# Operand splits queued behind weight splits, the first up weights staged earlier, the norm's factor and the conv rows computed later

## The chip, the cores and the metric

One Trainium2 chip, one core of it. The metric is device microseconds of one execution of the whole program. Engines are called as the profile calls them: PE (matmul), DVE, ACT, POOL and SP, which here issues most loads and stores.

## What is computed

One decoder layer on 512 prompt rows and 32 sample rows (544 columns). After retention, attention and the output projection, which the change leaves alone but for the tail of the projection, comes the feed-forward part:

```python
hp = hp + mixer_output(ro, rg, so, ret_gn_w[l], w_o[l], hp.dtype)
...
hn = rmsnorm(h, ffn_norm_w)
up = jnp.einsum('btd,df->btf', hn, w_up)              # 2048 -> 2 * 5632
g, u = jnp.split(up, 2, axis=-1)
gp = jnp.concatenate([conv_buf.astype(g.dtype), g], axis=1)
gc = conv_b + sum(gp[:, j:j + T] * conv_w[j] for j in range(CONV_W))
y = jnp.einsum('btf,fd->btd', jax.nn.silu(gc) * u, w_down)   # 5632 -> 2048
return y, gp[:, -(CONV_W - 1):]                        # the last two rows: "conv rows"
```

`rmsnorm` multiplies by the weight and by a factor per row, rsqrt(mean of squares + eps); the kernel applies the factor after the up product.

## The kernel before

**Precision.** All large products are made of two-part numbers: `hi` is a rounded copy that ACT makes (`act.copy`, L150), `lo = src - hi` comes from DVE (L151). Both parts of both sides are split; a product is hi·lo + lo·hi + hi·hi, three matmuls for each k of 128 rows. `split` does the two instructions.

**Units.** The up and down projections run in units (`unit`, L1112). A unit multiplies a 2x2 block matrix of weights by a 2x2 block of operands with seven products instead of eight. In the order of the program they are b11, t1, t2, b21, t3, b22, t4. For each, the weights (a raw block, or a sum of raw blocks that DVE makes at L1132, L1135, L1142, L1146) are split into one of three `uhi`/`ulo` buffers, in turn, and then multiplied (`product`, L1092) by the split operand of the same name in `xop`. A product takes 24 matmuls with 8 k's and 21 with 7. The results leave PSUM through ACT copies (`tu`, `p5`, `us`) and DVE adds. Work of the neighbouring unit (`todo`) is put between the products: `run(1)` after b11, `run(6)` after t2, `run(2)` after b21, `run(3)` after b22.

**The stages.** The output projection's second half (L1025 to L1042) ends at its sixteenth pass, i = 15; each pass loads weights into `raw` (three buffers, as `whi` and `wlo` have, in the pool `wp`), splits them, multiplies, adds the residue (`x1`), scales, stores `x1`, makes the operands of the up units (`build_x`) and sums the squares in `ssq`. After it four wide splits make the operands of b21 and t4 from `C` (L1043 to L1045). The pools `tb1` (`t1k`, two `x1`, `sq2`) and `wp` are closed and `ua` lies where they were; `ub` lies where `C` was. Pools lay their buffers out in the order of first use: in `ua` `us`, `g`, `tu` come first (8.8 KB of a partition), then three `uraw` of 4 KB; `tb1` is 7.6 KB and `wp` lies above it. A buffer waits only for the old buffers that it overlaps. `rstd_ffn` computes the norm's factor: two matmuls with `onesD` over `ssq`, then Ln, Exp and five DVE instructions. It is in the first unit's `run(2)`.

44 up units follow (`up_pair`), each with its conv, gate and, every second one, `blocks`, which stores the down operands in DRAM (`hx_keep`). Then the down units: three chunks of 8, 7 and 7 k's, eight units each. At the last unit ahead of a chunk, after each product, `fill` loads the operand of that name for the next chunk into the `lo` buffer (POOL's queue, L1224) and splits it there in two steps of up to four k's. `conv_rows` transposes the conv rows on PE in the first chunk's units 1 to 5.

**Order.** The kernel is written in Tile: a scheduler orders each engine's instructions ahead of time by priority and by when it expects them ready. On the chip each engine runs its list strictly in that order. The order in the trace can so differ from the order in the source.

I name the four places where a stage ends: T1 (output projection to up), B2 (up to the first down chunk), B3 and B4 (to the second and third chunk). A name with a prime (b11', t1') is a product of the first unit behind such a place.

Of the kernel before, what the change touches and what calls it, by code (L numbers as in the profile page):

```python
# [106 lines left out]
def trunk_kernel(  # L107
# [39 lines left out]
        return wp.tile([128, 8, 128], F32, name="raw", tag="raw")  # L147

    def split(hi, lo, src, eng=dve):
        act.copy(out=hi, in_=src)  # L150
        eng.tensor_tensor(out=lo, in0=src, in1=hi.bitcast(F32), op=sub)  # L151

    def stage_half(load, q, eng=dve):
        raw = wraw()
# [871 lines left out]
    for i in range(KT):  # L1026
        m = i // 2 + 8 * (i % 2)
        acc = half_project(m, 1, A_hi[:, 0:8], A_lo[:, 0:8])
        x1 = tb1.tile([128, 2, HC], F32, name="x1", tag="x1", bufs=2)
        dve.tensor_tensor(out=x1, in0=acc, in1=C[:, m], op=add)  # L1030
        act.activation(out=C[:, m], in_=x1, func=AF.Copy, scale=ffnw[:, m:m + 1])
        sth(out=x1_keep[m], in_=x1)
        if i % 2 == 0:
            split_x("b11", m, C[:, m, 0])
        else:
            build_x(i // 2)
        if i == 0:
            act.activation(out=ssq, in_=x1, func=AF.Square)
        else:
            sq = tb1.tile([128, 2, HC], F32, name="sq2", tag="sq2", bufs=1)  # L1040
            act.activation(out=sq, in_=x1, func=AF.Square)
            pool.tensor_tensor(out=ssq, in0=ssq, in1=sq, op=add)  # L1042
    for u in range(2):  # L1043
        for k in range(0, 8, 4):
            split(A_hi[:, k:k + 4, u], A_lo[:, k:k + 4, u], C[:, k + 8:k + 12, u])  # L1045
    tst.close()
    wst.close()
    ost.close()


    ust, ust2, upst = ExitStack(), ExitStack(), ExitStack()
    ps = upst.enter_context(tc.tile_pool(name="ps3", bufs=2, space=PSUM, reuse_waits="tile"))
    ua = ust.enter_context(tc.tile_pool(name="ua", bufs=1, reuse_waits="tile"))
    cst.close()
    ub = ust2.enter_context(tc.tile_pool(name="ub", bufs=1, side="right", reuse_waits="tile"))

    def ring(name, shape, dtype, n_a, n_b):
        turn_ = [0]

        def take():  # L1060
            i = turn_[0] % (n_a + n_b)
            turn_[0] += 1
            p, n = (ua, n_a) if i < n_a else (ub, n_b)
            return p.tile(shape, dtype, name=name, tag=name, bufs=n)
        return take

# [5 lines left out]
    new_cv = ring("cv", [128, 562], F32, 0, 1)  # L1072
    new_tu = ring("tu", [128, 2, HC], F32, 1, 1)
    new_us = ring("us", [128, 2, 2, HC], F32, 1, 0)
    new_p5 = ring("p5", [128, HC], F32, 0, 1)
    new_tt = ring("tt", [128, 3, HC], F32, 0, 1)

    def rstd_ffn():
        vb, tb = new_g()[:, 0:544].rearrange("p (u c) -> p u c", u=2), new_cv()[:, 0:544].rearrange("p (u c) -> p u c", u=2)
        for u in range(2):  # L1080
            pm = small2(ps)
            pe.matmul(pm[:, :HC], lhsT=onesD, rhs=ssq[:, u, :], start=True, stop=True)
# [6 lines left out]
    def b44(a):  # L1089
        return a.rearrange("p u (b t) -> p u b t", t=4)  # L1090

    def product(bank, w, x, first, last, parts=None):  # L1092
        n = w.shape[1]
        hi, lo = new_hi()[:, :n], new_lo()[:, :n]
        split(hi, lo, w)
        xh, xl = xop[x]
        for ks in parts or (range(n),):
            for k in ks:
                pe.matmul(bank, lhsT=hi[:, k], rhs=xl[:, k], start=(first and k == 0), stop=False, skip_group_check=True)  # L1099
                pe.matmul(bank, lhsT=lo[:, k], rhs=xh[:, k], start=False, stop=False, skip_group_check=True)  # L1100
# [3 lines left out]
    def unit(load, us, todo, joined, sign=1.0, behind={}, parts=None):  # L1104


        def run(when):
            for part in todo.get(when, ()):
                part()

        def prod(*a):
            product(*a, parts=parts)  # L1112
# [5 lines left out]
        tu, p5 = new_tu(), new_p5()  # L1118

        def out(dst, src):  # L1120
            if sign == 1.0:
                act.copy(out=dst, in_=src)  # L1122
            else:
                act.activation(out=dst, in_=src, func=AF.Copy, scale=sign)  # L1124

        a11, a21, a22 = load(0, 0), load(1, 0), load(1, 1)
        prod(bx, a11, "b11", True, False)
        act.copy(out=tu[:, 0], in_=bx)
        run(1)
        n = a11.shape[1]  # L1130
# [12 lines left out]
        prod(bx, a21, "t3", False, False)  # L1143
        out(us[1], bx)
# [8 lines left out]
    ups = {}  # L1153

    def load_up(f):
        def load(i, q):
            raw = new_raw()
# [2 lines left out]
        return load  # L1160

    def up_pair(f, todo, behind={}):
        if f % 2 == 0:
            ups["us"] = new_us()
        us2 = ups["us"]
        us = us2[:, f % 2]
        g = new_g()

        def joined(zy, tu):
            pool.memset(g[:, 0:2], 0.0)  # L1170
            pool.tensor_copy(out=g[:, 514:562].rearrange("p (b x) -> p b x", x=6)[:, :, 0:2],
                             in_=stT[:, :, f].rearrange("p (b r) -> p b r", r=2))
# [4 lines left out]
            dve.tensor_tensor(out=gs, in0=gs, in1=b44(rstd_bc[:, :, 256:272]), op=mult)  # L1177

        def conv():
            pool.tensor_copy(out=co[:, 0:2, f], in_=g[:, 512:514])  # L1180
            pool.tensor_copy(out=co[:, 2:18, f].rearrange("p (b r) -> p b r", r=2), in_=g[:, 514:562].rearrange("p (b x) -> p b x", x=6)[:, :, 4:6])
            cv = ups["cv"] = new_cv()
# [5 lines left out]

        def gated():
            cv = ups["cv"]  # L1190
            dve.tensor_tensor(out=us, in0=us, in1=rstd_bc, op=mult)  # L1191
            dve.scalar_tensor_tensor(out=us[:, :, 0:256], in0=us[:, :, 0:256], scalar=-1.0, in1=halves_of(cv[:, 0:512]), op0=mult, op1=mult)
            uss = b44(us[:, :, 256:272])
# [2 lines left out]
        def blocks():  # L1196

            j = f // 2
            tt = new_tt()
            for op, src in ((0, us2[:, 0, 0]), (5, us2[:, 1, 1]), (3, us2[:, 1, 0])):  # L1200
                sth(out=hx_keep[op][:, j], in_=src)
# [6 lines left out]
            sth(out=hx_keep[6][:, j], in_=tt[:, 1])  # L1208
            sth(out=hx_keep[1][:, j], in_=tt[:, 2])

        unit(load_up(f), (us[:, 0], us[:, 1]), todo, joined, behind=behind, parts=None if f else (range(7), range(7, 8)))
        return {1: [conv], 6: [gated], 2: [blocks] if f % 2 else []}


# [2 lines left out]
    chunks = ((0, 8), (8, 7), (15, 7))  # L1217

    def fill(c, name):
        def go():  # L1220
            j0, n = chunks[c]
            hi, lo = xop[name]
            raw = lo.bitcast(F32)
            sth(out=raw[:, :n], in_=hx_keep[order7.index(name)][:, j0:j0 + n])  # L1224
            for h in range(0, n, 4):
                p = slice(h, min(h + 4, n))
                if name == "t2":
# [4 lines left out]
        return go  # L1232

    def fills(c):
        return {name: fill(c, name) for name in order7} if c < len(chunks) else {}

    def emit_y(m, y):
        yp = new_g()[:, 0:512].rearrange("p (c d) -> p c d", c=4)
# [12 lines left out]
    def down_pair(c, mp, todo):  # L1251
# [24 lines left out]
        unit(load, (y[:, 1, 0], y[:, 1, 1]), todo, joined, sign=-1.0, behind=fills(c + 1) if mp == 7 else {})  # L1276
        return {6: [finish_y if last else keep_y]}

    todo = {2: [rstd_ffn]}
    for f in range(FT):  # L1280
        todo = up_pair(f, todo, behind=fills(0) if f == FT - 1 else {})

    def conv_rows(q):
        def go():
            n = min(4, 18 - 4 * q)
            cob = new_g()[:FT, 0:512].rearrange("p (i c) -> p i c", c=128)
            pt = small2(ps)
            for i in range(n):
                pe.transpose(out=pt[:FT, 128 * i:128 * i + 128], in_=co[:, 4 * q + i, :], identity=ident)
# [49 lines left out]
```

## Time and profile before

| | us |
|---|---|
| median of 3 runs | 2242.22 (2238.29 to 2245.8) |
| profiled execution, its own time | 2239.99 |
| its span, first to last instruction | 2238.2 |
| PE busy | 2176.6 (97%) |
| DVE busy | 1630.1 (73%) |
| ACT busy | 1010.7 (45%) |
| POOL busy | 291.9 (13%) |
| mean granted TensorE clock | 0.986 of full speed |

The page cuts the span into 40 slices of 56 us. PE's busy digit is 9 in nearly all, DVE's is 8 through the up stage; the granted clock is 8 or 9 tenths in the first slices, in those around 760, 1710, 1910 and 2050 us, and at the end. Matmuls are pipelined and a busy PE isn't a PE at its peak, so the count of matmuls in a stretch says more than the busy time. DMA moves 128 GB/s in the mean; the highest slice, the first, has 289 GB/s, and a store of `x1` (272 KB) takes 2.4 us from issue to landing. Durations of single instructions include a tenth of a microsecond in which the next one already runs.

### The profile page before, as it was taken

Reading aid. Unit: us, or ns where it says so; the run is one execution under the profiler, and the core shown is the slowest. Engines: PE = TensorE matmul, PEld = TensorE weight load, DVE = VectorE, ACT = ScalarE, POOL = GpSimd, SP = SyncE. Lnnn points to the kernel's source line nnn. Section 1 sums busy time; section 2 is a strip of 40 time slices with the busy share of each in tenths; the row PEclk is TensorE's granted clock in tenths of the full one; section 3 lists DMA queues with packets and bytes.
Section 4 is the critical chain, followed back from the end, with each engine's and each line's share of the span. In section 5 each row is a group of like instructions: output and inputs, shape, how many; then the busy total and the mean of one; then the engine's idle time right before and its main releaser. Section 6 shows DMA issues by size and latency. Waiting matters only on the chain.

```text
span 2238.2 us, 42004 instructions
## 1 busy us (share of the span) xinstructions
PE 2176.6 (97%) x17159; PEld 2139.1 (96%) x17159; DVE 1630.1 (73%) x2457; ACT 1010.7 (45%) x1612; POOL 291.9 (13%) x463
## 2 busy tenths in 40 slices
PE   7999999999999799999999999999998999898998
PEld 7999999999999799999999999999998999898998
DVE  5555557875437778888888888888888767767775
ACT  5122235566215544444444444444445445445444
POOL 1000000000003212122122122122122101001000
PEclk8999999999999899999999999999998999999999
DMA  9333343324644343343443443434436656557553
GB/s 289 100 97 94 87 88 77 82 67 120 130 115 136 112 124 114 113 145 107 121 137 113 124 125 116 133 114 126 124 116 224 149 128 194 139 131 221 140 150 98
DMA packets 452656, 286.52 MB, mean 128 GB/s; under 512 B 46320, under 2 KB 430640, under 8 KB 452080
## 3 DMA queue, kind: packets, MB, share of 16 engines
q1 hardware_dynamic: 433376, 222.16, 36.6%
q0 software_dynamic: 19088, 61.68, 9.1%
q8 instruction: 134, 2.20, 0.4%
q14 instruction: 58, 0.48, 0.1%
HBM read 231.38 MB, written 47.67 MB: 125 GB/s over the span
## 4 chain that ended last, share of the span: by engine, by line
PE 64%; issue 18%; DVE 9%; DMA 6%; POOL 2%; ACT 1%; SPq 1%; DVEq 0%; POOLq 0%; ACTq 0%
PE acc L174 17%; PE acc L178 9%; PE bx L1100 7%; PE bx L1099 6%; PE bx L1102 6%; PE zy L1099 5%; PE zy L1100 5%; PE zy L1102 4%; DMA uraw<-in_w_up_dram 3%; DVE ulo L151 3%; DMA A_lo<-hx_keep 1%; POOL x_keep L1267 1%; DVE cv L1186 1%; DVE us L1191 1%; PE sm L686 1%
## 5 line engine op out<-in xcount | busy, mean ns | idle before, releaser
L151 DVE TENSOR_TENSOR ulo<-uraw,uhi 128x1024 fp32r<-128x1024 f32 (+1 forms) x272 | 322.1, 1188 | 87.3 <-ACT uhi L150 87.0
L150 ACT CAST uhi<-uraw 128x1024 fp32r<-128x1024 f32 (+1 forms) x272 | 278.2, 1023 | 108.6 <-issue 72.2
L150 ACT CAST uhi<-usum 128x1024 fp32r<-128x1024 f32 (+1 forms) x204 | 209.3, 1026 | 227.0 <-DVE usum L1135 123.4
L1100 PE MATMUL bx<-X_hi,ulo 128*128 128x272 f32 x1056 | 277.2, 294 | 11.6 <-DVE ulo L151 11.4
L174 PE MATMUL acc<-A_lo,whi 128*128 128x272 f32 x1344 | 286.2, 294 | 1.4 <-DVE A_lo L290 0.8
L1099 PE MATMUL bx<-X_lo,uhi 128*128 128x272 f32 x1056 | 275.2, 291 | 9.7 <-ACT uhi L150 9.7
L174 PE MATMUL acc<-A_hi,wlo 128*128 128x272 f32 x1344 | 280.6, 290 | 0.0
L151 DVE TENSOR_TENSOR ulo<-usum,uhi 128x1024 fp32r<-128x1024 f32 (+1 forms) x204 | 242.6, 1189 | 47.3 <-ACT uhi L150 47.3
L1099 PE MATMUL bx<-A_lo,uhi 128*128 128x272 f32 x1056 | 271.0, 289 | 4.7 <-ACT us L1122 2.2
L1099 PE MATMUL zy<-A_lo,uhi 128*128 128x272 f32 x1056 | 272.5, 290 | 1.3 <-ACT p L1124 0.5
L1100 PE MATMUL zy<-A_hi,ulo 128*128 128x272 f32 x1056 | 271.4, 289 | 0.6 <-DVE ulo L151 0.6
L1100 PE MATMUL bx<-A_hi,ulo 128*128 128x272 f32 x1056 | 270.1, 287 | 0.0
L150 ACT CAST whi<-raw 128x1024 fp32r<-128x1024 f32 x100 | 104.8, 1048 | 279.4 <-PE acc L178 234.2
L174 PEld LDWEIGHTS acc<-A_lo,whi 128*128 128x128 f32 x1344 | 211.8, 189 | 7.9 <-issue 4.2
L1100 PEld LDWEIGHTS bx<-X_hi,ulo 128*128 128x128 f32 x1056 | 202.3, 192 | 16.5 <-DVE ulo L151 16.2
L174 PEld LDWEIGHTS acc<-A_hi,wlo 128*128 128x128 f32 x1344 | 211.9, 189 | 0.8
L1099 PEld LDWEIGHTS bx<-X_lo,uhi 128*128 128x128 f32 x1056 | 201.9, 191 | 11.0 <-ACT uhi L150 10.9
L1099 PEld LDWEIGHTS bx<-A_lo,uhi 128*128 128x128 f32 x1056 | 199.2, 189 | 5.8 <-ACT us L1122 2.4
L1099 PEld LDWEIGHTS zy<-A_lo,uhi 128*128 128x128 f32 x1056 | 199.7, 189 | 2.5 <-ACT p L1124 1.1
L1100 PEld LDWEIGHTS zy<-A_hi,ulo 128*128 128x128 f32 x1056 | 199.6, 189 | 0.8 <-DVE ulo L151 0.8
L1100 PEld LDWEIGHTS bx<-A_hi,ulo 128*128 128x128 f32 x1056 | 198.9, 188 | 0.0
L178 PE MATMUL acc<-A_hi,whi 128*128 128x272 f32 x1344 | 187.6, 290 | 0.0
(437 smaller groups left out, 4256.6 us busy)
## 6 DMA issues: line engine op xcount, KB each, us to landing
uraw<-in_w_up_dram SPq DMA_DIRECT2D x176, 512.0 KB
uraw<-in_w_down_dram SPq DMA_DIRECT2D x64, 448.0 KB
raw<-in_w_in_dram SPq DMA_DIRECT2D x52, 512.0 KB
uraw<-in_w_down_dram SPq DMA_DIRECT2D x32, 512.0 KB
hx_keep<-us POOLq DMA_DIRECT2D x88, 136.0 KB, 2.0
hx_keep<-tt POOLq DMA_DIRECT2D x66, 136.0 KB, 4.8
x_keep<-us POOLq DMA_DIRECT2D x32, 272.0 KB, 5.1
raw<-in_w_in_dram SPq DMA_DIRECT2D x32, 256.0 KB
```

The lines of the kernel that those rows point to most:

```text
L150: act.copy(out=hi, in_=src)
L151: eng.tensor_tensor(out=lo, in0=src, in1=hi.bitcast(F32), op=sub)
L174: pe.matmul(acc[:, u, :HC], lhsT=w, rhs=x[:, u, :], start=(first and i == 0 and w is wh), stop=False)
L178: pe.matmul(acc[:, u, :HC], lhsT=wh, rhs=xh[:, u, :], start=False, stop=(last and i == n - 1))
L686: pe.matmul(po[:, 256 * kv:256 * kv + 256], lhsT=vS[:, n if n == 0 else n - 1 + kb, kv, :], rhs=t[:, kb, :], start=(j == 0), stop=(j == le ...
L1099: pe.matmul(bank, lhsT=hi[:, k], rhs=xl[:, k], start=(first and k == 0), stop=False, skip_group_check=True)
L1100: pe.matmul(bank, lhsT=lo[:, k], rhs=xh[:, k], start=False, stop=False, skip_group_check=True)
L1102: pe.matmul(bank, lhsT=hi[:, k], rhs=xh[:, k], start=False, stop=(k == n - 1), skip_group_check=True)
L1186: dve.scalar_tensor_tensor(out=cva, in0=g[:, 0:560], scalar=w0[:, f:f + 1], in1=cva, op0=mult, op1=add)
L1191: dve.tensor_tensor(out=us, in0=us, in1=rstd_bc, op=mult)
L1267: sth(out=x1_keep[2 * mp + i], in_=y[:, i], accum_op=add)
```

## The change

1. `split` returns its two instructions. At the end of a chunk the loads stay behind the products; the splits of the new operands move into the next chunk's first unit, each traced right behind the split of that product's weights, with `tc.issue_after` on both of its instructions: on ACT and on DVE they can't be issued ahead of them. b11's operand alone is split at the end of the last unit, behind t4's weights.
2. The first up unit's b11 weights are loaded and split as a seventeenth pass of the output projection's staging, in `raw`, `whi`, `wlo`. `ua` is opened behind that product; its a11 is loaded again, for the sums. The four wide splits of b21's and t4's operands come behind the product t1.
3. `rstd_ffn` moves from `run(2)` to `run(3)` and takes its constant from a copy (`held`) that POOL makes behind the write of `tu`. `conv_rows` moves one unit later, its identity held in the same way.
4. `us` and `g` are taken later, `p5` moves from `ub` to `ua`: the first buffers of `ua` are now the three `uraw`.

```diff
     def split(hi, lo, src, eng=dve):
-        act.copy(out=hi, in_=src)
-        eng.tensor_tensor(out=lo, in0=src, in1=hi.bitcast(F32), op=sub)
+        a = act.copy(out=hi, in_=src)
+        return a, eng.tensor_tensor(out=lo, in0=src, in1=hi.bitcast(F32), op=sub)
...
         acc = half_project(m, 1, A_hi[:, 0:8], A_lo[:, 0:8])
+        if i == KT - 1:
+            first_w = stage_half(cols_of(w_up[0], 0), 0)
...
-    for u in range(2):
-        for k in range(0, 8, 4):
-            split(A_hi[:, k:k + 4, u], A_lo[:, k:k + 4, u], C[:, k + 8:k + 12, u])
-    tst.close()
-    wst.close()
     ost.close()
...
-    ua = ust.enter_context(tc.tile_pool(name="ua", bufs=1, reuse_waits="tile"))
-    cst.close()
-    ub = ust2.enter_context(tc.tile_pool(name="ub", bufs=1, side="right", reuse_waits="tile"))
+    ua, ub = [], []
+
+    def open_ua():
+        tst.close()
+        wst.close()
+        ua.append(ust.enter_context(tc.tile_pool(name="ua", bufs=1, reuse_waits="tile")))
+
+    def last_x():
+
+        for u in range(2):
+            for k in range(0, 8, 4):
+                split(A_hi[:, k:k + 4, u], A_lo[:, k:k + 4, u], C[:, k + 8:k + 12, u])
+        cst.close()
+        ub.append(ust2.enter_context(tc.tile_pool(name="ub", bufs=1, side="right", reuse_waits="tile")))
...
-    new_p5 = ring("p5", [128, HC], F32, 0, 1)
+    new_p5 = ring("p5", [128, HC], F32, 1, 0)
...
+    def held(src, behind):
+
+        t = new_tt()[:, 0, 0:128]
+        pool.tensor_copy(out=t, in_=behind)
+        pool.tensor_copy(out=t, in_=src)
+        return t
+
     def rstd_ffn():
+        mean = held(onesD, ups["tu"][:, 0, 0:128])
...
-    def product(bank, w, x, first, last, parts=None):
-        n = w.shape[1]
-        hi, lo = new_hi()[:, :n], new_lo()[:, :n]
-        split(hi, lo, w)
+    def product(bank, w, x, first, last, parts=None, between=None):
+        if isinstance(w, tuple):
+            hi, lo = w
+        else:
+            hi, lo = new_hi()[:, :w.shape[1]], new_lo()[:, :w.shape[1]]
+            ups["split"] = split(hi, lo, w)
+        if between:
+            between()
+        n = hi.shape[1]
...
-        a11, a21, a22 = load(0, 0), load(1, 0), load(1, 1)
-        prod(bx, a11, "b11", True, False)
+        if first_w is None:
+            a11, a21, a22 = load(0, 0), load(1, 0), load(1, 1)
+            prod(bx, a11, "b11", True, False)
+        else:
+            prod(bx, first_w, "b11", True, False)
+            open_ua()
+            a11, a21, a22 = load(0, 0), load(1, 0), load(1, 1)
+        tu, p5 = new_tu(), new_p5()
+        ups["tu"] = tu
...
     def fills(c):
-        return {name: fill(c, name) for name in order7} if c < len(chunks) else {}
+
+
+        if c >= len(chunks):
+            return {}
+        now = {}
+
+        def pinned(convert):
+            def go():
+                a, d = ups["split"]
+                with tc.issue_after(a.ins), tc.issue_after(d.ins):
+                    convert()
+            return go
+
+        steps = [fill(c, name) for name in order7]
+        for i, name in enumerate(order7):
+            now[name] = steps[i][0]
+            if i:
+                late[name] = pinned(steps[i][1])
+
+        def end():
+            steps[6][0]()
+            pinned(steps[0][1])()
+
+        now["t4"] = end
+        return now
...
-    todo = {2: [rstd_ffn]}
+    todo, late = {3: [rstd_ffn]}, {}
     for f in range(FT):
-        todo = up_pair(f, todo, behind=fills(0) if f == FT - 1 else {})
+        todo = up_pair(f, todo, behind={"t1": last_x} if f == 0 else fills(0) if f == FT - 1 else {})
...
+            if q == 0:
+                ups["ident"] = held(ident, ups["tu"][:, 0, 0:128])
...
-            if c == 0 and 1 <= mp < 6:
-                todo[3] = [conv_rows(mp - 1)]
+            if c == 0 and 2 <= mp < 7:
+                todo[3] = [conv_rows(mp - 2)]
```

## Rows read from the trace of the kernel before

**Rows 1.** Busy time by stretch: length, busy us (instructions) by engine, granted clock, DMA.

```profile
592.00:670.00 78.00, 78.00 (x623) 78.00 (x622) 27.28 (x39) 15.38 (x15) 0.00 (x0) 1.00 0.60 140
...
757.00:800.00 43.00, 31.40 (x214) 29.43 (x213) 34.17 (x42) 22.35 (x29) 5.13 (x7) 0.84 0.47 129
1690.00:1750.00 60.00, 50.52 (x356) 49.25 (x356) 53.19 (x61) 35.85 (x45) 13.80 (x21) 0.89 0.69 222
1900.00:1950.00 50.00, 42.16 (x296) 41.33 (x297) 35.61 (x37) 21.95 (x32) 3.48 (x4) 0.90 0.58 152
2040.00:2080.00 40.00, 31.16 (x220) 29.56 (x219) 33.64 (x34) 24.52 (x33) 9.11 (x11) 0.94 0.86 255
```

**Rows 2.** Waits from 757 to 815 us: who waited for whom, us, times, longest.

```profile
PE bx L1099 <- ACT uhi L150: 5.5, 1, 5.5
...
PE sm L1082 <- POOL rstd_bc L1042: 4.8, 1, 4.8
```

**Rows 3.** Timeline at T1: start, length, engine, line, operation, [idle before <- releaser].

```profile
760.95 0.72 DVE L1030 TENSOR_TENSOR x<-acc,C 128x544 f32<-128x544 f32 x1
...
761.96 0.56 POOL L1032 DMA_DIRECT2D x_keep<-x  x1 [4.76 <-DVE x L1030]
...
771.09 1.03 ACT L150 CAST uhi<-uraw 128x1024 fp32r<-128x1024 f32 x1
...
782.13 0.39 ACT L1122 COPY p<-zy 128x272 f32<-128x272 f32 x1 [0.38 <-PE zy L1102]
...
798.72 0.36 ACT L1122 COPY us<-bx 128x272 f32<-128x272 f32 x1
```

**Rows 4.** Waits of SP's load queue from 735 to 815 us.

```profile
SPq L165 <- PE acc L178: 15.3, 1, 15.3
...
SPq L165 <- DVE A_lo L151: 9.8, 1, 9.8
```

**Rows 5.** Timeline, DVE: two operand splits in two steps each, 8 and 7 k's.

```profile
1717.67 2.49 DVE L151 TENSOR_TENSOR A_lo<-A_lo,A_hi 128x1088 fp32r<-128x1088 f32 x2 [0.55 <-ACT A_hi L150]
...
1902.30 2.21 DVE L151 TENSOR_TENSOR A_lo<-A_lo,A_hi 128x1088 fp32r<-128x1088 f32 x2 [0.77 <-ACT A_hi L150]
```

**Rows 6.** Timeline at B2: b21's fill, an operand cast, b11' weights, t4' result.

```profile
1702.76 0.91 POOL L1224 DMA_DIRECT2D A_lo<-hx_keep  x1 [2.48 <-PE zy L1099]
...
1706.43 2.11 ACT L150 CAST X_hi<-X_lo 128x1088 fp32r<-128x1088 f32 x2 [3.75 <-DMA X_lo<-hx_keep]
...
1720.79 1.22 DVE L151 TENSOR_TENSOR ulo<-uraw,uhi 128x1024 fp32r<-128x1024 f32 x1
...
1750.61 0.40 ACT L1124 ACTIVATE us<-bx 128x272 f32<-128x272 f32 x1 [1.90 <-PE bx L1102]
```

**Rows 7.** Timeline at B3: b21's fill, b11' cast and lo, last operand's cast, t4' result.

```profile
1888.72 0.98 POOL L1224 DMA_DIRECT2D A_lo<-hx_keep  x1 [2.47 <-PE zy L1099]
...
1896.39 0.93 ACT L150 CAST uhi<-uraw 128x896 fp32r<-128x896 f32 x1
...
1904.43 1.08 DVE L151 TENSOR_TENSOR ulo<-uraw,uhi 128x896 fp32r<-128x896 f32 x1
...
1907.62 1.88 ACT L150 CAST A_hi<-A_lo 128x1088 fp32r<-128x1088 f32 x2 [1.49 <-DMA A_lo<-hx_keep]
...
1931.46 0.40 ACT L1124 ACTIVATE us<-bx 128x272 f32<-128x272 f32 x1 [1.69 <-PE bx L1102]
```

**Rows 8.** Timeline at B4: b21's fill, b11' weights' lo part, t4' result.

```profile
2051.76 0.98 POOL L1224 DMA_DIRECT2D A_lo<-hx_keep  x1 [2.09 <-PE zy L1099]
...
2064.42 1.09 DVE L151 TENSOR_TENSOR ulo<-uraw,uhi 128x896 fp32r<-128x896 f32 x1
...
2092.63 0.40 ACT L1124 ACTIVATE us<-bx 128x272 f32<-128x272 f32 x1 [1.69 <-PE bx L1102]
```

**Rows 9.** Busy time by stretch, as rows 1, around two gaps of PE.

```profile
764.00:778.00 14.00, 7.35 (x25) 6.03 (x26) 11.13 (x17) 8.43 (x11) 1.55 (x3) 0.51 0.61 161
...
2064.00:2066.00 2.00, 0.44 (x3) 0.44 (x4) 1.50 (x2) 0.00 (x0) 0.00 (x0) 1.00 1.05 353
```

More of the change, by code (lines that the diff above doesn't have):

```diff
@@ L1062, in take @@
             turn_[0] += 1
-            p, n = (ua, n_a) if i < n_a else (ub, n_b)
+            p, n = (ua[0], n_a) if i < n_a else (ub[0], n_b)
             return p.tile(shape, dtype, name=name, tag=name, bufs=n)
@@ L1081, in rstd_ffn @@
             pm = small2(ps)
-            pe.matmul(pm[:, :HC], lhsT=onesD, rhs=ssq[:, u, :], start=True, stop=True)
+            pe.matmul(pm[:, :HC], lhsT=mean, rhs=ssq[:, u, :], start=True, stop=True)
             dve.tensor_scalar(out=vb[:, u, :], in0=pm[:, :HC], scalar1=EPS, scalar2=None, op0=add)
@@ L1102, in product, with unit @@
                 pe.matmul(bank, lhsT=hi[:, k], rhs=xh[:, k], start=False, stop=(k == n - 1), skip_group_check=True)
-    def unit(load, us, todo, joined, sign=1.0, behind={}, parts=None):
+    ups = {}
+    def unit(load, us, todo, joined, sign=1.0, behind={}, parts=None, within={}, first_w=None):
         def run(when):
@@ L1111, in prod @@
         def prod(*a):
-            product(*a, parts=parts)
+            product(*a, parts=parts, between=within.get(a[2]))
             if a[2] in behind:
@@ L1117, in unit @@
         zy = ps.tile([128, 2, 512], F32, name="zy", tag="zy", bufs=2)[:, :, :HC]
-        tu, p5 = new_tu(), new_p5()
         def out(dst, src):
@@ L1143, in unit @@
         prod(bx, a21, "t3", False, False)
+        us = us() if callable(us) else us
         out(us[1], bx)
@@ L1151, in unit @@
         joined(zy, tu)
-    ups = {}
     def load_up(f):
@@ L1162, in up_pair, with result @@
     def up_pair(f, todo, behind={}):
[L1163 to L1167, printed above, removed]
+        def result():
+            if f % 2 == 0:
+                ups["us"] = new_us()
+            return ups["us"][:, f % 2, 0], ups["us"][:, f % 2, 1]
         def joined(zy, tu):
+            g = ups["g"] = new_g()
             pool.memset(g[:, 0:2], 0.0)
@@ L1179, in conv @@
         def conv():
+            g = ups["g"]
             pool.tensor_copy(out=co[:, 0:2, f], in_=g[:, 512:514])
@@ L1190, in gated @@
             cv = ups["cv"]
+            us = ups["us"][:, f % 2]
             dve.tensor_tensor(out=us, in0=us, in1=rstd_bc, op=mult)
@@ L1198, in blocks @@
             j = f // 2
+            us2 = ups["us"]
             tt = new_tt()
@@ L1209, in blocks @@
             sth(out=hx_keep[1][:, j], in_=tt[:, 2])
-        unit(load_up(f), (us[:, 0], us[:, 1]), todo, joined, behind=behind, parts=None if f else (range(7), range(7, 8)))
+        unit(load_up(f), result, todo, joined, behind=behind, parts=None if f else (range(7), range(7, 8)), first_w=None if f else first_w)
         return {1: [conv], 6: [gated], 2: [blocks] if f % 2 else []}
@@ L1219, in fill, with load, convert @@
     def fill(c, name):
[L1220 to L1224, printed above, removed]
+        j0, n = chunks[c]
+        hi, lo = (t[:, :n] for t in xop[name])
+        raw = lo.bitcast(F32)
+        def load():
+            sth(out=raw, in_=hx_keep[order7.index(name)][:, j0:j0 + n])
+        def convert():
             for h in range(0, n, 4):
@@ L1231, in go @@
                     split(hi[:, p], lo[:, p], raw[:, p])
-        return go
+        return load, convert
     def fills(c):
-        return {name: fill(c, name) for name in order7} if c < len(chunks) else {}
+        if c >= len(chunks):
[17 more added lines that the diff above has]
+        return now
     def emit_y(m, y):
@@ L1274, in finish_y @@
                 emit_y(2 * mp + i, y[:, i])
-        unit(load, (y[:, 1, 0], y[:, 1, 1]), todo, joined, sign=-1.0, behind=fills(c + 1) if mp == 7 else {})
+        within = dict(late)
+        late.clear()
+        unit(load, (y[:, 1, 0], y[:, 1, 1]), todo, joined, sign=-1.0, behind=fills(c + 1) if mp == 7 else {}, within=within)
         return {6: [finish_y if last else keep_y]}
-    todo = {2: [rstd_ffn]}
+    todo, late = {3: [rstd_ffn]}, {}
     for f in range(FT):
-        todo = up_pair(f, todo, behind=fills(0) if f == FT - 1 else {})
+        todo = up_pair(f, todo, behind={"t1": last_x} if f == 0 else fills(0) if f == FT - 1 else {})
     def conv_rows(q):
@@ L1288, in go @@
             for i in range(n):
-                pe.transpose(out=pt[:FT, 128 * i:128 * i + 128], in_=co[:, 4 * q + i, :], identity=ident)
+                pe.transpose(out=pt[:FT, 128 * i:128 * i + 128], in_=co[:, 4 * q + i, :], identity=ups["ident"])
             act.copy(out=cob[:, 0:n], in_=pt[:FT, 0:128 * n].rearrange("p (i c) -> p i c", i=n))
```

## The prediction

> **What bounds the kernel now.** I read the page's slices first: PE is busy nearly everywhere, so the time is PE's matmuls plus the places where it runs thin. Then the stretches around those places. At full speed PE does 623 matmuls in 78 us, 7.99 each us [rows 1]; so a product of 24 takes 3.0 us, one of 21 takes 2.63 us. The four stage ends do 214, 356, 296 and 220 matmuls in 43, 60, 50 and 40 us, where 343, 479, 399 and 320 would fit [rows 1]: 129 + 123 + 103 + 100 = 455 missing matmuls, 57 us. Some of that is the granted clock, 0.84 to 0.94 there [rows 1]. All that the change can earn lies in these 57 us; a change of under 0.3% (6.7 us) could not be told from none.
>
> What ends last differs. At T1 PE waits 4.8 us for the squares' sum, then 5.5 us for the first up weights [rows 2]: their cast starts at 771.09, though PE could have gone on at 759.7, where SP's wait for the last matmuls ends (744.4 + 15.3) [rows 3, 4]. At B2, B3 and B4 DMA is busy 0.69, 0.58 and 0.86 of the stretch [rows 1], but data isn't the last thing: at B3 b11' has its weights cast by 1897.3 and gets their lo part only at 1904.43, and the last operand's cast starts at 1907.62, long before its product is due [rows 7]. DVE took operand splits first, which were needed 3 to 6 products later. The same at B2, where the lo part comes at 1720.79, and at B4, at 2064.42 [rows 6, 8]. ACT meanwhile sits 3.75 us at an operand's cast whose load hasn't landed [rows 6], with t4's weights queued behind it. So these three are a matter of order on DVE and ACT, with a floor set by DVE's amount of work.
>
> **Part 1, the splits behind their weights.** Nothing is removed; the work moves into the next chunk's first unit, in the order in which PE needs it. I count DVE's work from the end of t4's weight split and let DVE run without a break; PE's last product t4' then starts when the first half of its operand is split.
>
> B2: b21 has released its lo buffer at 1702.76 [rows 6]; its hi·hi third takes 8 more matmuls, 1.0 us, so t4's weights may be cast at 1703.8 and are split by 1706.0 (1.03 and 1.22 us, [rows 3, 6]). DVE then has seven operand splits of 2.5 us [rows 5], 17.4; seven weight splits, 8.5; four sums at the same price, 4.9; two half-wide adds, 0.9; and of the last up pair's gate eight instructions about as wide as the 0.72 us one [rows 3], 5.8: 37.5 us. Less the second half of the last split, 1.25, t4' starts at 1742.3 and ends at 1745.3. Before it ends at 1750.6 [rows 6]: **5.3 us** gained. PE needs 21 us for that unit and DVE over 35, so PE stays the one that waits, 1 to 3 us a product.
>
> B3: b21's lo at 1888.72 [rows 7], done 1889.7, t4's weights split by 1892.0. DVE: seven operand splits of 2.2 us [rows 5], 15.5; seven weights and four sums of 1.08 us [rows 7], 11.9; adds and the join, 1.6: 29 us. t1's weights need the buffer that b22 holds until 1895.7, and their cast takes 0.93 us [rows 7]: 1.3 us of DVE idle. 1892.0 + 29 + 1.3 - 1.1 = 1921.2; with 2.63 us, 1923.9, where before has 1931.5 [rows 7]: **7.6 us**.
>
> B4: b21's lo at 2051.76 [rows 8], done 2052.65, t4's split by 2054.7; + 29 + 0.9 - 1.1 + 2.63 = 2086.1, where before has 2092.6 [rows 8]: **6.5 us**.
>
> The cover: the last operand has landed by 1907.62 at B3 [rows 7], and its split is due at about 1918; t1's and t2's have some 5 us to spare. Were a load later, ACT would wait at its cast with the next weights behind it, a microsecond lost for each late. On POOL the loads keep their places. What is given up is DVE's free time in the last unit of a stage, where two or three operands were split before; the count has that in it, since it starts at 1706.0 with all but b11's still to do.
>
> The clock: a gap can bring it down. At T1 it reads 0.51 over 14 us [rows 9]. At B4 PE is busy 0.44 of 2 us and the clock still reads 1.00 [rows 9]. At half clock a product takes 5.4 us (24 matmuls at half of 7.99), close to DVE's 5.2 us a product (37.5 / 7) and over its 4.2 at B3, so a drop under a DVE-bound unit costs about 1 us, not the 2.4 of the product; ends 0 and the whole unit, below. I take 1 us at each: 4.3 + 6.6 + 5.5 = **16.4 us**.
>
> **Part 2, the first up weights.** In `raw`, `whi` and `wlo` they need only the buffers of pass 13, long free by the last pass; their 1.03 and 1.22 us on ACT and DVE lie under PE's matmuls. b11' starts at 759.7 and ends at 762.7, in time that PE now idles. Then something else is late: t1's weights. The new order of `ua` puts `uraw` at the bottom, where two of the three now lie over `x1`, `sq2` and `t1k`, still in use by pass 15; before, SP's second load was released by PE at 759.7 [rows 4]. The add that makes `x1` runs at 760.95, behind a wide split [rows 3]; without that split at 759.8. Its store follows by a microsecond [rows 3] and lands 2.4 us later, so SP may load from about 763.8. Two blocks of 512 KB at 289 GB/s and 1.4 us of latency (2.4 us less 272 KB at that rate) land at 769; sum, cast and lo part put t1 at 771.3 to 772.5, at the half clock that follows such a gap [rows 9], done by 777.5. Before, it is done at 782.1 [rows 3]. Five products more, 15.1 us, and 1.1 for the factor's matmuls: 793.7 against 798.7 [rows 3], 5.0 us. The a11 loaded twice costs 1.8 us if SP takes it first. The splits of b21's and t4's operands find ACT and DVE free between 764 and 769; were they behind t1's, `ub`, for which SP now waits 9.8 us [rows 4], would open 3 us later. Ends 0 and 8 (all of the 8.2 us gap after b11' filled); I take **4 us**, near the 5.0.
>
> **Part 3, factor and conv rows.** The factor's two matmuls leave the gap but keep out of PE's way; some 3 us of DVE and two table loads fall into a unit in which DVE's busy digit is 8, hidden by up to two products split ahead; the next unit reads the result only in its conv. `held` adds two small POOL copies. 0, or 3 us if the lead is used up. The conv rows' transposes can't stand in PE's list ahead of b11' any more; there PE would have waited for b11' lo part anyway [rows 6]: 0, already in the count.
>
> **The sum.** 4 + 16.4 = 20.4 us. From the profiled execution's own 2240.0 that is 2219.6; that execution lies 2.2 us under the median of the runs. I say **2220**.
>
> **The rivals.**
> *Half clock through the unit.* If bursts of a product with a wait behind each keep the clock down, seven products take 38 us (B2) and 33.2 (B3, B4): t4' ends at 1749.8, 1932.0 and 2093.8 against 1750.6, 1931.5 and 2092.6, a loss of 0.9 us in all, and the 4 us of T1 leave 2237. Against it: the 1.00 at a PE busy for 0.44 of 2 us; for it: 0.51 at T1 [rows 9]. [...]
>
> *The scheduler's order is what it was.* If the pinned splits only replace an order that costs as much, the three stage ends stay, and T1's ends of 0 to 4 leave 2236 to 2240. Against: a weight split ready 7 us and not issued [rows 7].
>
> *Slower: splits behind result copies.* ACT also copies each product out of PSUM and waits for PE there. If the scheduler sets the copy of product n ahead of the operand cast for product n + 1, each product pays half a cast and half a split, 2.4 us (2.2 with 7 k's), after the one before. It decides by the clock: at full speed B3 would end at 1898.7 + 2.63 + 6 x 4.83 = 1930.3, as before; at half, 1898.7 + 4.75 + 6 x 6.95 = 1945.2. With half clock all through, B2, B3 and B4 lose 13.6 + 13.7 + 14.3, less 4: 2278. For it: ACT waits in order, as the 3.75 us show [rows 6]. Against: before, weight casts run products ahead of the copies (b11' cast at 1896.39, PE then still in t4) [rows 7].
>
> **How the numbers follow.** The forecast, 2205 to 2233 by its bounds (T1 0 to 8, no clock loss to 2.4 us at each end, 3 us for a used lead, DVE less densely packed): 0.72. Half clock: 0.12. Old order: 0.07. Slower: 0.09. The range that holds 8 in 10 runs from 2205 to 2240, through the first three less a little on both sides. Faster by over 0.3% (below 2233): 0.74, the forecast and 0.02 of a half clock that holds in part; same: 0.16, the rest of that rival and most of the old order; slower: 0.10.
>
> **What would show it.** In the profile after: b11' of the up stage directly behind the last projection matmul, and the gap behind it, 8 us, ended by `usum` and not by the factor; ACT's casts at B2 to B4 in pairs, weights then operand, none waiting for DMA; PE's waits there on DVE's operand lo parts, 1 to 3 us each; t4' ends at about 1742, 1917 and 2072 on its own scale. Wrong would be a granted clock of 0.5 over the whole first unit, ACT copies between weight cast and operand cast, or loads landing behind their casts.

## The result and the profile after

The changed kernel takes 2256.61 us (median of 6 runs, 2255.6 to 2262.27); beside it the kernel before took 2239.6 (6 runs, 2235.69 to 2245.8). The ratio is 1.008 with an interval of 1.0061 to 1.0099: slower by 0.8%, 17 us. The forecast was 2220, faster than before. The profiled execution took 2262.27 us, its span is 2260.5, its mean granted clock 0.982.

The stretches of [rows 1], after the change: length, busy us (instructions) of PE, PEld, DVE, ACT, POOL, granted clock, DMA share, GB/s.

```profile
592.00:670.00 78.00, 78.00 (x624) 78.00 (x623) 27.62 (x40) 15.97 (x16) 0.33 (x1) 1.00 0.60 139
...
757.00:800.00 43.00, 29.29 (x195) 27.43 (x194) 31.40 (x39) 20.76 (x27) 3.34 (x7) 0.80 0.51 141
1690.00:1750.00 60.00, 43.88 (x321) 42.33 (x320) 48.25 (x56) 31.90 (x41) 14.21 (x20) 0.89 0.62 208
1900.00:1950.00 50.00, 37.69 (x272) 36.31 (x272) 36.97 (x38) 25.61 (x36) 5.81 (x7) 0.90 0.67 179
2040.00:2080.00 40.00, 32.56 (x260) 32.34 (x259) 20.21 (x22) 17.40 (x25) 9.13 (x11) 0.97 0.84 254
```

Full speed is what it was, 624 matmuls in 78 us. T1, B2 and B3 do 195, 321 and 272 matmuls where they did 214, 356 and 296. B4 looks better, 260 against 220, but only since its gap now begins at 2072.6 and reaches beyond 2080. DVE is busy for less than before at T1, B2 and B4: it stands still, though the forecast had it run without a break.

The timeline shows at what. Start, length, engine, line, operation, [idle before <- releaser], at B2, B3 and B4:

```profile
1728.11 1.23 DVE L1161 TENSOR_TENSOR usum<-uraw 128x1024 f32<-128x1024 f32 x1 [10.06 <-DMA uraw<-in_w_down_dram]
...
1914.81 1.09 DVE L1161 TENSOR_TENSOR usum<-uraw 128x896 f32<-128x896 f32 x1 [11.65 <-DMA uraw<-in_w_down_dram]
1915.82 0.72 DVE L1322 TENSOR_TENSOR us<-zy,tu 128x544 f32<-128x544 f32 x1
1916.45 1.08 DVE L151 TENSOR_TENSOR ulo<-usum,uhi 128x896 fp32r<-128x896 f32 x1
1917.45 2.20 DVE L151 TENSOR_TENSOR X_lo<-X_lo,X_hi 128x1088 fp32r<-128x1088 f32 x2
...
1918.79 0.59 PE L1120 MATMUL zy<-X_lo,uhi 128*128 128x272 f32 x1 [9.81 <-DVE X_lo L151]
...
2058.72 19.34 SPq L1318 DMA_DIRECT2D uraw<-in_w_down_dram  x3
...
2086.29 1.09 DVE L1161 TENSOR_TENSOR usum<-uraw 128x896 f32<-128x896 f32 x1 [18.00 <-DMA uraw<-in_w_down_dram]
...
2089.64 0.60 PE L1120 MATMUL zy<-X_lo,uhi 128*128 128x272 f32 x1 [17.07 <-DVE X_lo L151]
```

L1161 is the first weight sum of a unit. The one that waits here belongs to the second unit of the chunk; it is traced one unit ahead. In DVE's list it now stands ahead of the lo part of t1' of the first unit (1916.45) and of t1's operand (1917.45), for which PE waits. Its own weights are loaded by SP while POOL's queue loads the seven operands, which at B4 are issued from 2053.43 to 2069.23. While these loads fill the DMA engines, three load issues of SP's take 19.34 us. Before, the same sum stood behind operand splits, at 1912.41 and 2079.41 in that trace.

To see what each place costs I count in each profile from the same matmul, the 5701st (some 724 us after the first; the time up to it, which no edit touches, varies between 716.8 and 725.6 us over the profiles below), to the last ACT copy of `us` of a unit, and take the difference from the kernel before. T1 is the first up unit, "up" the next 42, B2 the last up unit and two down units, B3 and B4 the eight units from there to the second one of the next chunk; us, less is faster:

| kernel | T1 | up | B2 | B3 | B4 | end |
|---|---|---|---|---|---|---|
| forecast | -4 | 0 | -4.3 | -6.6 | -5.5 | -20.4 |
| changed | +2.3 | -0.2 | +4.6 | +3.4 | +12.3 | +22.6 |
| e1 late sum | +0.8 | +1.3 | -5.4 | -5.9 | -5.7 | -14.7 |
| e10 the same again | +1.6 | -1.4 | -5.5 | -5.9 | -5.2 | -16.3 |
| e2 Part 1 alone | +0.3 | +2.4 | +5.6 | +3.3 | +14.0 | +25.5 |
| e3 without Part 1 | +0.9 | +0.8 | -1.2 | +0.3 | +0.4 | +1.4 |
| e4 small loads | +1.9 | -1.2 | -6.1 | -6.6 | -4.0 | -15.9 |
| e5 t1k first | -2.5 | -1.7 | -5.5 | -5.9 | -5.6 | -21.2 |
| e11 the same again | -1.4 | +0.4 | -5.5 | -5.9 | -4.5 | -16.7 |
| e6 and a11 last | -4.2 | -0.6 | -5.0 | -5.9 | -4.3 | -20.0 |
| e7 uraw above | -2.8 | +4.1 | -5.3 | -6.3 | -3.6 | -14.0 |
| e8 Part 1, late sum | +0.2 | +3.9 | -4.5 | -7.9 | -6.4 | -14.7 |
| e9 untied | +0.3 | -0.8 | -4.4 | -2.8 | -5.2 | -12.6 |

"up" scatters from -1.7 to +4.1, in e2 and e8 by +2.4 and +3.9 with the code of before: under 4 us at the end of one profile say nothing. Where kernels have the same code, B2 and B3 repeat within 0.5 us; T1 and B4 scatter by some 2 us (T1 from +0.3 to +2.3, B4 from -3.6 to -5.7).

B3's column holds a part that isn't the stage end's. In every kernel with the later conv rows the third to seventh unit of the first chunk take 1.1 to 1.5 us longer, in e2 and e8 0.1.

### The profile page after: what moved, and what is told of

The parts are those of the page before. It is cut to its first block, busy times and chain, and to the rows that moved or that the text cites. A ratio compares the mean times of both kernels' runs of the same rounds, so it can differ in the third digit from the quotient of the medians.

```text
span 2260.5 us, 42011 instructions
## 1 busy us (share of the span) xinstructions
PE 2174.0 (96%) x17159; PEld 2137.6 (95%) x17159; DVE 1629.9 (72%) x2457; ACT 1010.1 (45%) x1612; POOL 293.8 (13%) x467
## 5 line engine op out<-in xcount | busy, mean ns | idle before, releaser
L1121 PE MATMUL bx<-X_hi,ulo 128*128 128x272 f32 x1048 | 271.3, 291 | 4.3 <-DVE ulo L151 4.1
L1120 PEld LDWEIGHTS bx<-X_lo,uhi 128*128 128x128 f32 x1048 | 198.2, 189 | 16.7 <-DVE X_lo L1264 15.1
```

## The experiments

**e1: the sum moved, nothing else.** `late_sum` is true for the second unit of each chunk alone; its sum comes behind the split of that unit's own b11 weights.

```diff
-        dve.tensor_tensor(out=s1, in0=a21, in1=a22, op=add)
+        with tc.issue_after(ups["split"][1].ins) if late_sum else ExitStack(): dve.tensor_tensor(out=s1, in0=a21, in1=a22, op=add)
```

> The changed kernel with one more instruction held back: DVE's first weight sum of a chunk's second unit (traced one unit ahead, in the list of the first unit) stands behind the split of that second unit's first weights, instead of ahead of the lo part of t1' of the first unit. Theory A (the changed kernel's DVE waits 10.1, 11.7 and 18.0 us at B2, B3 and B4 for a load that only the next unit needs, and everything of the first unit stands behind it): these three waits go, PE's waits of 11.7, 9.8 and 17.1 us on lo parts fall under 4 us each, and the time falls 25 to 38 us under the changed kernel's 2256.6, to 2219 to 2232. Rival B (the load that this sum waits for is late for all, and the splits behind weights are what costs): the same idle time comes back as waits of ACT or DVE for other loads or for operand splits, and the time stays within 8 us of the changed kernel. Rival C (half clock through the first unit): the waits go, the granted clock stays near half over the unit, and about half of the gain, 12 to 18 us, is seen.

Measured: 2224.25 us, ratio to before 0.9923 (0.99 to 0.9946), 32 us under the changed kernel; the second time 2221.94, 0.9908 (0.989 to 0.9926). The sums and PE's waits, first the timeline, then the waits at B3 (1885 to 1935 us) and B4 (2035 to 2075; who waited for whom: us, times, longest):

```profile
1737.15 2.36 DVE L1161 TENSOR_TENSOR usum<-uraw 128x1024 f32<-128x1024 f32 x2
...
1911.14 2.09 DVE L1161 TENSOR_TENSOR usum<-uraw 128x896 f32<-128x896 f32 x2
...
2066.42 1.09 DVE L1161 TENSOR_TENSOR usum<-uraw 128x896 f32<-128x896 f32 x1
```

```profile
PE bx L1120 <- DVE X_lo L1264: 1.5, 1, 1.5
...
PE bx L1120 <- DVE X_lo L1264: 1.9, 1, 1.9
```

and the same two stretches by engine:

```profile
1885.00:1935.00 50.00, 45.35 (x348) 43.64 (x347) 42.09 (x43) 27.65 (x38) 7.02 (x8) 1.00 0.70 190
2035.00:2075.00 40.00, 34.06 (x263) 32.76 (x262) 36.56 (x39) 26.18 (x36) 10.55 (x8) 1.00 0.83 265
```

The sum runs without a wait. PE's longest wait on an operand is 1.5 us at B3 and 1.9 us at B4 (at B2 it is 2.5 us), DVE is busy 36.56 of 40 us at B4, and the granted clock reads 1.00 in both stretches (0.97 from 1690 to 1750 us, at B2). Theory A holds; the rivals of late loads for all and of half clock don't.

**e2 and e3: Part 1 alone, and all but Part 1.** e2 is the kernel before with the late, tied splits; e3 the changed kernel with the `fill` of before (load and split both right behind the product).

> The kernel before with Part 1 alone: operand splits tied behind the weight splits of the next chunk's first unit; first up weights, norm's factor and conv rows as before. Theory A: the whole loss comes from B2 to B4 and is here as well: 15 to 20 us slower than before, T1 unchanged, DVE waiting 10 us and more for the next unit's weights at each of the three places. Rival (T1 or the later factor and conv rows carry the loss): within 5 us of before.

> The changed kernel with the operand splits of before, right behind the products they follow; first up weights, norm's factor and conv rows as in the change. Theory A: B2 to B4 as before, T1 about 1.5 us longer, so within 4 us of before. Rival (T1 or the later factor and conv rows carry the loss): 10 to 17 us slower than before. The prediction's own Part 2 would make it 4 us faster.

Measured: e2 2261.72 us, ratio 1.0089 (1.0071 to 1.0107); e3 2240.04, ratio 0.9991 (0.9979 to 1.0003). All of the loss is Part 1's: B2 to B4 cost 22.9 us in e2, and the sum waits as in the changed kernel, up to 11.0 us at B2, 12.4 at B3 and 18.5 at B4, here from 2030 to 2118 us:

```profile
DVE usum L1134 <- DMA uraw<-in_w_down_dram: 20.7, 3, 18.5
```

e3 is the price of Parts 2 and 3 together: nothing that the runs can tell from zero. In its profile T1 is 0.9 us longer, and the second to seventh unit of the first chunk, with the later conv rows, are 1.3 us longer.

**e4: small operand loads.** The order on DVE at B3 and B4 stays as in the changed kernel (at B2 it shifts a little); only the bytes go.

```diff
-            sth(out=raw, in_=hx_keep[order7.index(name)][:, j0:j0 + n])
+            sth(out=raw[:, :2], in_=hx_keep[order7.index(name)][:, j0:j0 + 2])
```

> The changed kernel, but each load of a new chunk's operand brings 2 of its 8 (7) blocks: three quarters of the operands' bytes at B2 to B4 are left out, and what the down products multiply there is partly not the operand. Order of instructions at B3 and B4 as in the changed kernel. Theory A with starved loads (the weights of the next unit come late since the operands' loads fill the DMA engines): DVE's waits at its sum fall from 10 to 18 us to under 3 us, and the time falls 25 to 35 us under the changed kernel. Rival (the sum waits for a buffer or for its place in SP's list, whatever the operands' bytes): the waits stay over 8 us and the time within 8 us of the changed kernel.

Measured: 2224.75 us, 32 us under the changed kernel. An operand is 272 KB in place of 952 (1088 at B2). The sum waits not at all, 0.94 and 0.53 us, where it waited 10.06, 11.65 and 18.00. Load sizes (from 2020 to 2060 us: count, KB each, median us to landing), and the three sums:

```profile
A_lo<-hx_keep POOLq DMA_DIRECT2D x4, 272.0 KB, 4.2
```

```profile
1716.75 1.22 DVE L1161 TENSOR_TENSOR usum<-uraw 128x1024 f32<-128x1024 f32 x1
...
1890.57 1.09 DVE L1161 TENSOR_TENSOR usum<-uraw 128x896 f32<-128x896 f32 x1 [0.94 <-DMA uraw<-in_w_down_dram]
...
2045.27 1.09 DVE L1161 TENSOR_TENSOR usum<-uraw 128x896 f32<-128x896 f32 x1 [0.53 <-DMA uraw<-in_w_down_dram]
```

So it takes both: the sum ahead of what PE needs, and operand loads that keep its weights from coming. Either alone gone, the loss is gone.

**e9: the same late splits, not tied.**

```diff
-                a, d = ups["split"]
-                with tc.issue_after(a.ins), tc.issue_after(d.ins):
-                    convert()
+                convert()
```

> The changed kernel with its operand splits traced just as late, but not tied: both issue_after edges left out. In this program the scheduler then sets some operand splits ahead of weight splits again, and the next unit's first sum stands behind the operand split of t1' and later, no more ahead of the lo part of t1'. Theory A (the tie itself was harmless; what costs is that with it the sum moved to the front of DVE's list): the waits of 10 to 18 us go, and the time is under the changed kernel's 2256.6 by 12 us or more, between the kernel before and the run with the late sum: 2225 to 2243. Rival (the ties, or late tracing, cost by themselves): within 6 us of the changed kernel.

Measured: 2228.61 us, ratio 0.9935 (0.9918 to 0.9952), 28 us under the changed kernel. Without the ties some operand splits go ahead of weight splits again, and the sum comes behind them: at B4 it starts at 2078.21 and waits for nothing.

```profile
2078.21 1.08 DVE L1161 TENSOR_TENSOR usum<-uraw 128x896 f32<-128x896 f32 x1
```

Tracing the splits later brings most of the gain. The ties are what moved the sum forward. That the scheduler did so since it took the sum's weights for loaded is likely, but no run shows what it assumed. B3 gains 2.8 us here and 5.9 with the tie and the late sum, and e10, run on the same chip as e9, is 6.7 us faster (2221.94): the tie is worth something once the sum is out of the way.

**e8: Part 1 with the late sum, on the kernel before.**

> The kernel before with Part 1 and the late sum; first up weights, norm's factor and conv rows as before. Theory A: what the prediction gave Part 1, 16.4 us, is what B2 to B4 now bring: 14 to 19 us faster than before, T1 within 1 us of before. Rival (the gain of the run with the late sum came in part from the later factor and conv rows): under 12 us.

Measured: 2221.52 us, ratio 0.9912 (0.9883 to 0.9942), B2 to B4 -18.8 us, T1 +0.2. It is 19.9 us under the kernel before, a little more than the 14 to 19 expected. The gain of e1 is Part 1's alone; of the 1.8 us by which these columns beat e1's, most is the conv rows' 1.5.

**e5, e6, e7 and the repeats: T1.** In the changed kernel the first load behind b11' has two waits. The waits of SP's queue there (755 to 800 us), then the timeline:

```profile
SPq L165 <- DMA x_keep<-x: 24.7, 1, 24.7
...
SPq L165 <- DVE X_lo L151: 2.5, 1, 2.5
```

```profile
759.05 1.29 DVE L151 TENSOR_TENSOR A_lo<-C,A_hi 128x1088 fp32r<-128x1088 f32 x1 [2.05 <-ACT A_hi L150]
760.26 0.72 DVE L1032 TENSOR_TENSOR x<-acc,C 128x544 f32<-128x544 f32 x1
760.89 1.28 DVE L151 TENSOR_TENSOR A_lo<-C,A_hi 128x1088 fp32r<-128x1088 f32 x1
...
764.65 1.28 DVE L151 TENSOR_TENSOR A_lo<-C,A_hi 128x1088 fp32r<-128x1088 f32 x1
765.86 0.43 DVE L151 TENSOR_TENSOR X_lo<-t1k,X_hi 128x272 fp32r<-128x272 f32 x1
...
766.31 14.54 SPq L165 DMA_DIRECT2D uraw<-in_w_up_dram  x8
...
770.61 2.18 PE L1098 MATMUL sm<-rstd_bc,tt 128*128 128x272 f32 x4 [8.61 <-POOL tt L1090]
...
774.57 1.23 DVE L1161 TENSOR_TENSOR usum<-uraw 128x1024 f32<-128x1024 f32 x1 [1.29 <-DMA uraw<-in_w_up_dram]
...
776.92 0.59 PE L1120 MATMUL zy<-X_lo,uhi 128*128 128x272 f32 x1 [4.13 <-ACT uhi L150]
```

Behind the store of `x1` (up to 766.31 - 2.5 = 763.8) the load waits 2.5 us more, for the last read of `t1k`, which ends at 765.86 + 0.43. Two wide splits stand between `x1` and that read, and one more ahead of `x1` (759.05). e5 ties the wide splits behind it (`x7`: `t1k`'s last split); e6 does the same and loads a21 and a22 ahead of a11:

```diff
+                with tc.issue_after(x7[0].ins), tc.issue_after(x7[1].ins):
                     split(A_hi[:, k:k + 4, u], A_lo[:, k:k + 4, u], C[:, k + 8:k + 12, u])
...
-            a11, a21, a22 = load(0, 0), load(1, 0), load(1, 1)
+            a21, a22, a11 = load(1, 0), load(1, 1), load(0, 0)
```

e7 has e6's order of loads, ties the wide splits behind the split of t1's weights, takes `us`, `g` and `tu` first in `ua`, so that `uraw` lies above `t1k` as before, and holds the factor's constant behind `tu[:, 1]`:

```diff
+        ups["us"], ups["vb"], ups["tu"] = new_us(), new_g(), new_tu()
...
-        mean = held(onesD, ups["tu"][:, 0, 0:128])
+        mean = held(onesD, ups["tu"][:, 1, 0:128])
```

> The kernel with the late sum, and at T1 the four wide splits of b21's and t4's operands tied behind the last split of t1k, in place of between the steps that make it. Theory D (the changed kernel's first uraw load waits for the last read of t1k, which stands behind two wide splits on DVE; it starts 0.03 us after that read ends): the load starts 2.4 us earlier, counted from the last projection matmuls, and the first up unit ends 2 to 3 us earlier than with the late sum alone. Rival E (the loads are behind the store of x1, as the prediction had it): load and unit end where they did, within 0.5 us. Medians: 2 to 3 us under the run with the late sum, 2221 to 2222, or the same.

> As the one before, and the three loads behind the first up product in the order a21, a22, a11 instead of a11, a21, a22: t1's sum needs the first two alone. If the load of a11, 512 KB, is a term of its own (1.8 us at 289 GB/s), t1's sum starts 1.5 to 3 us earlier than in the one before, and the first up unit ends 4 to 6 us earlier than with the late sum alone. Rival: the sum is then held by DVE's four wide splits, which stand ahead of it, and the gain is under 1 us.

> The kernel with the late sum, and at T1 the first buffers of ua as in the kernel before (us, g and tu first, so that the three uraw lie above t1k, x1 and sq2), loads in the order a21, a22, a11, the four wide splits tied behind the split of t1's weights, and the factor's constant held behind the second half of tu instead of the first, which puts its two matmuls behind the unit's last products. Theory D: no load waits for t1k; t1's weights are there within 2 us of the end of b11', and the first up unit ends 7 to 11 us earlier than with the late sum alone; median 2213 to 2218. Rival F (the unit is bound by DVE and ACT, which do the wide splits, sums and splits of the unit one after the other): the unit starts earlier and ends within 3 us of the late sum alone; median 2221 to 2225.

Measured: e5 2217.74 us, ratio 0.9892 (0.9864 to 0.992); e6 2220.57, 0.9902 (0.9875 to 0.9928); e7 2223.25, 0.9921 (0.9896 to 0.9945). T1 ends 3.3 us (e5), 5.0 (e6) and 3.6 (e7) earlier than in e1. In e5's timeline the load still starts as `t1k`'s read ends:

```profile
752.28 0.72 DVE L1033 TENSOR_TENSOR x<-acc,C 128x544 f32<-128x544 f32 x1 [2.04 <-PE acc L178]
753.83 0.44 DVE L1016 TENSOR_TENSOR C<-C 128x272 f32<-128x272 f32 x1 [0.82 <-ACT C L1034]
...
757.23 0.43 DVE L151 TENSOR_TENSOR X_lo<-t1k,X_hi 128x272 fp32r<-128x272 f32 x1
757.69 13.54 SPq L165 DMA_DIRECT2D uraw<-in_w_up_dram  x8
```

So the releaser is as theory D has it. Its price is near: counted from the 5701st matmul the load starts at 39.4 us, where it starts at 41.25 in the six kernels whose T1 is that of the changed kernel: 1.9 us earlier, not 2.4. Of these, 1.2 come from the add that makes `x1`, which no longer stands behind a wide split; from that add to the load it is 5.4 us, where it was 6.05. t1' then starts 2.4 us earlier than in e1 and the unit ends 3.3 us earlier; the difference is within the 2 us by which T1 scatters.

In e6, with a11 loaded last, t1's sum starts 1.5 us earlier than in e5, as expected, but t1' only 0.5 us. The unit ends 1.7 us earlier than in e5 and 2.8 earlier than in e11, near that scatter, and the medians show no gain: what loading a11 last is worth is not shown. e7 missed: t1' starts 9.2 us earlier than in e1, but the unit doesn't end 7 to 11 us earlier. A wait of SP's queue in e7, then three stretches at T1:

```profile
SPq L165 <- DVE A_lo L151: 13.1, 1, 13.1
```

```profile
753.00:761.00 8.00, 5.14 (x42) 4.92 (x40) 5.09 (x11) 3.03 (x7) 2.08 (x2) 1.00 0.55 165
761.00:771.00 10.00, 5.29 (x24) 4.77 (x24) 9.35 (x8) 6.01 (x7) 0.00 (x0) 0.66 0.03 7
771.00:781.00 10.00, 8.82 (x47) 8.51 (x48) 5.96 (x6) 3.79 (x5) 0.58 (x2) 0.66 1.17 295
```

DVE is busy 9.35 of the 10 us behind the first, four wide splits in a row; DMA has nothing to do (0.03), since SP waits 13.1 us for these splits: the next loads go to `ub`, which they hold; and the clock reads 0.66 for 20 us. The gap went to another place: close to rival F, with 3.6 us at the unit's end where it had at most 3, and a median inside its range.

> The kernel with the late sum once more, beside the next one on the same chip, for their difference: 2219 to 2228, as the first time.

> The kernel with the late sum and the wide splits behind the last split of t1k once more. If T1's 3.3 us, counted from the last projection matmuls, is all that it brings: 2 to 5 us under the one before this; if the 6.5 us seen at the end of its profile are all its own: 5 to 8 us.

On the same chip: e10 2221.94 us, e11 2220.54, ratio 0.9911 (0.9889 to 0.9932). The 1.4 us between them is less than the runs can tell, and neither range that was expected holds. e11's profile again has T1 earlier, by 3.0 us against e10; in the medians this is not shown. All versions with the late sum beat both kernels, with medians of 2218 to 2224 us.

## Why the prediction was wrong

**Part 1, the step that failed: "let DVE run without a break".** The count took four sums at 1.08 us each and asked of the first unit's loads alone whether they had landed. In the changed kernel two of the four that DVE does there, the first and the third of a unit (L1161 and L1171), belong to the unit behind. The first unit's own were done before: at B3, L1161 at 1882.52 and L1171 at 1885.30. SP loads the weights of that next unit while seven operands of 952 KB go through the same DMA engines. [rows 1] showed the stretch at B4 at 0.86 of DMA, and the text said "data isn't the last thing". That held for the first unit's data. The sentence "were a load later, ACT would wait [...] a microsecond lost for each late" put the risk on the wrong engine at a tenth of its size: DVE waited, 10.06, 11.65 and 18.00 us, with the splits of the unit in progress behind it.

**Its total came out close, in part by luck.** With that sum out of the way B2, B3 and B4 gain 17.0 us (e1) and 16.6 (e10) where the sum said 16.4. But the forecast was for the end of t4'. Up to there, over the last unit of a stage and the first of the next, e1 gains 6.6, 10.1 and 9.2 us where the sum said 4.3, 6.6 and 5.5. With the late sum DVE does only two sums between t4's weight split and t4', not four: at B3 the stretch from 1882.4 to 1908.7 takes 26.3 us, where the count had 29.2 (1892.0 to 1921.2). The microsecond taken for the clock isn't seen at B3 and B4, where it reads 1.00. Then the second unit, with its sum late, gives back 1.1, 2.7 and 2.9 us (in e4, which has the sum early, it is 0.1 to 0.5 us faster than before), and 2.1 us lie in the units between, 1.5 of them with the conv rows. PE waits less than the "1 to 3 us a product": 4.6 us in all at B3 and 3.0 on operands and weights at B4. So work by row times count was a usable price of DVE's part, a little high; the order of DVE's list was assumed, and what the second unit would pay was left out. The two ends of that stretch in e1 are b11's operand split, right behind t4's weights, and the start of t4':

```profile
1882.36 2.20 DVE L151 TENSOR_TENSOR X_lo<-X_lo,X_hi 128x1088 fp32r<-128x1088 f32 x2
...
1908.73 0.39 PE L1120 MATMUL bx<-A_lo,uhi 128*128 128x272 f32 x1 [0.44 <-DVE A_lo L151]
```

**The order.** The prediction took its order from the source, "the order in which PE needs it". A tie orders two instructions; it says nothing of a third one, and the third took the place that the tied ones had left. The rival "the scheduler's order is what it was" asked the right question, but had the old order as the worst there is; the new one costs 37 us more than the one counted (+20.3 against -17.0).

**The slower rival** had operand splits behind ACT's result copies and 2278 us. Slower came, but not so: PE waited for DVE's lo parts behind the sum, and in e1, with the same ties on ACT, B2 to B4 are faster.

**Half clock through the unit** didn't hold. In e1 PE waits up to 1.9 us between products at B3 and B4, the products of 21 taking 2.63 us, and the granted clock is 1.00. The Trainium skill, TensorE: Matmul & The Clock Gate, section HAM oscillation, tells of a kernel whose bursts of matmuls are each shorter than the wait for data behind them, and which starts every burst cold; the waits here are shorter than the bursts, so e1 is not that case. In the changed kernel the clock falls in the long gap at B4. Stretches of 2 us, with PE still since 2072.6:

```profile
2074.00:2076.00 2.00, 0.00 (x0) 0.00 (x0) 0.00 (x0) 0.00 (x0) 0.00 (x0) 1.00 1.03 359
2076.00:2078.00 2.00, 0.00 (x0) 0.00 (x0) 0.00 (x0) 0.00 (x0) 0.00 (x0) 0.92 1.06 340
2078.00:2080.00 2.00, 0.00 (x0) 0.00 (x0) 0.00 (x0) 0.00 (x0) 0.00 (x0) 0.50 1.08 233
```

One step of the working on half clock is wrong: 24 matmuls at half of 7.99 each us would take 6.0 us, not 5.4. The 5.4 itself fits the trace of the kernel before: around 775 us, where the clock is at half, matmuls start 0.227 us apart (24 x 0.227 = 5.4).

**Part 2** was sized at -4 and gave +0.3 to +2.3 (six profiles with this T1). b11' runs directly behind the projection, and the gap behind it is there: PE waits 8.61 and 4.13 us. "SP may load from about 763.8" is when the store lets go, within a microsecond (the two traces are shifted by 0.7 us). The second wait, 2.5 us for `t1k`, was missed, though the text names `t1k` among what lies under `uraw`. The wide splits were to "find ACT and DVE free between 764 and 769" and went ahead instead. The a11 loaded twice costs 1.8 us "if SP takes it first", the text says, and SP did take it first. So t1's sum starts at 774.57, where its data was to land at 769. With the wide splits and the order of the loads mended (e6) T1 gives 4.2 us in one profile.

**Part 3** cost nothing that the medians show (e3), as taken; the profiles have 1.3 us for the later conv rows. The factor's matmuls stood in PE's list ahead of t1', where the text had them out of the way, and the first gap ended with them, not with `usum`. They cost nothing only because t1's weights came 4.13 us later.

## What to carry to other kernels

Before an instruction is moved or tied, list what else stands in that engine's queue in the stretch, the work made ahead for the next unit too, and ask of each when its data lands; on an engine that runs in order the latest of them is the price, not its duration. Where DMA is near full, estimate how late a load can be that is issued among large ones by their bytes over the rate of the stretch (here 7 x 952 KB at about 350 GB/s, 19 us; the sum waited 18.00 us at B4, 10.06 and 11.65 at B2 and B3). And compare the order of a changed program with the old one before its work is counted: the one instruction that decided here is not in the diff.

## What the runs showed of the hardware

With the operand loads of POOL's queue under way, three load issues of SP's took 19.34 us at B4, the last of them alone 13.01. In e4, with small operands, the three took 5.84 us from the start of the first to the end of the last, mostly waits between them; the last alone took 0.37. From the changed kernel, then from e4:

```profile
2065.06 13.01 SPq L1318 DMA_DIRECT2D uraw<-in_w_down_dram  x1
```

```profile
2035.18 5.84 SPq L1318 DMA_DIRECT2D uraw<-in_w_down_dram  x3
...
2040.66 0.37 SPq L1318 DMA_DIRECT2D uraw<-in_w_down_dram  x1
```

So here the loads of another queue held up the issue itself, not just the landing; what the issue waited for, the traces don't say. In e1 the same issue stands as long, 14.98 us, and costs nothing, since no work that PE is waiting for stands behind its data. And the granted clock still read 1.00 from 2074 to 2076 us, with no matmul in those 2 us, before it fell to 0.50 (the three stretches above).
